# Finishing the early conditioning columns on ScalarE, and emitting each norm one tile later

## The chip, the cores and the metric

The kernel runs on 1 core of one Trainium2 chip. The metric is the device time of one execution in microseconds; before the change it is 2299.08 us (median of 3 runs, 2298.39 to 2300.27).

The core's engines run independently and meet at semaphores: TensorE (PE) multiplies, VectorE (DVE) and ScalarE (ACT) work elementwise, GpSimd (POOL) does little here, and SyncE (SP) issues nearly all the transfers. Each engine works through its own queue in order.

## The reference

Two decoder layers over 256 tokens of width 2048. Each layer has a token mixer (mLSTM in the first, forgetting attention in the second) and a SwiGLU network, each behind an RMSNorm that is modulated by a conditioning vector `c`:

```
cs = silu(c)
mod = cs @ ada_w[layer] + ada_b[layer]            # 6 vectors of 2048
sh1, sc1, g1, sh2, sc2, g2 = split(mod, 6)
h = rms_norm(x, norm_mix_w) * (1 + sc1) + sh1
x = x + g1 * mixer(h)
h = rms_norm(x, norm_ffn_w) * (1 + sc2) + sh2
x = x + g2 * swiglu(h)
```

A last RMSNorm closes it. All values are float32; matmuls use a value split into a high and a low part, three products for each.

## The kernel before

**Tiles.** Width 2048 is cut into 16 k-tiles of 128 partitions. `hT[:, k]` holds the modulated norm of k-tile `k`, transposed, as high and low parts for 256 tokens. A "unit" is 512 columns of the first projection `w_in`, over a range of k-tiles: `unit(i, ka, kb, ...)`, line 805. It fetches 1024 KB of weights (four k-tiles, `fetch`, L254), ACT casts them to the high part `hi` (L263), DVE subtracts for the low part `lo` (L264), and PE does 24 matmuls (L290 to L292), 12 for each half of the pair. Finished banks are copied out by `keep` (L800) and copied back as a start value (L812).

**Conditioning.** `mod` is computed by DVE, since `ada_w` would be used for only one row. For each of the 192 columns blocks `ada_tile` fetches 1024 KB and multiplies and sums it against `cs` in one instruction (L195) into one column of `acc`. `set_mods` adds the bias and, for a scale, multiplies by the norm's weight (L183 for a scale column, L189 for a shift column); the result stands in `mods`.

**The early stage.** The first norm needs scale (`SC1`) and shift (`SH1`) of layer 0, 32 products, before the first projection can use all of `hT`. So the kernel spreads these over the first units. The generator `early()` (L744) goes through k: product and column for `SC1`, a step ends; product and column for `SH1`, then the norm of tile k, a step ends. `norm_tile` (L378) consists of DVE `t` = x times scale times row norm (L382), ACT adds the shift and writes the high part of `hT` (L386), DVE writes the low part (L387). For k below 4 `norm_full` does the same with the full float32 value (L737, L741, L364, L365).

**Who advances it.** `upto(k)` runs the generator until k tiles of `hT` are emitted (`at[0]`), and `pace(1.0)` takes one step for each unit. Units 4 to 11 first use tiles 0 to 3, then units 0 to 11 tiles 4 to 7, then units 0 to 3 tiles 8 to 11. Each unit thus carries one product: two units make one k-tile of the norm.

**Order.** Up to L791 the instructions stand as written (a hand-kept order). After that a scheduler orders each engine's queue, so that an instruction may stand elsewhere than where the text emits it. Products and weights share a ring of five 1024 KB buffers (`rawp`); SP issues the next transfer when the buffer five back is free.

Of the kernel before, what the change touches and what calls it, by code (L numbers as in the profile page):

```python
# [12 lines left out]
AF = mybir.ActivationFunctionType  # L13
ALU = mybir.AluOpType
# [6 lines left out]
KT = D // P  # L21
# [10 lines left out]
def kernel(  # L32
# [5 lines left out]
    nc = tc.nc  # L38
# [45 lines left out]
    for j in range(3):  # L84
        nc.gpsimd.affine_select(
            out=sel, in_=sel, pattern=[[-1, 16]], compare_op=ALU.not_equal,
# [5 lines left out]
        out=mask, in_=mask, pattern=[[-1, P]], compare_op=ALU.is_ge,  # L92
# [74 lines left out]
    SH1, SC1, G1, SH2, SC2, G2 = range(6)  # L167


    for layer in range(2):  # L170
        for vec, nw in ((SC1, nw_mix), (SC2, nw_ffn)):
            b = adb[layer][:, 16 * vec : 16 * vec + 16]
            nc.vector.scalar_tensor_tensor(
                out=b, in0=b, scalar=1.0, in1=nw[layer], op0=ALU.add, op1=ALU.mult
            )

    def set_mods(layer, vec, k0, n):
        j = slice(16 * vec + k0, 16 * vec + k0 + n)
        m, a, b = mods[layer][:, j], acc[layer][:, j], adb[layer][:, j]
        if vec in (SC1, SC2):  # L180
            nw = (nw_mix if vec == SC1 else nw_ffn)[layer][:, k0 : k0 + n]
            if n == 1:
                nc.vector.scalar_tensor_tensor(  # L183
                    out=m, in0=a, scalar=nw, in1=b, op0=ALU.mult, op1=ALU.add
                )
                return
            nc.vector.tensor_tensor(m, a, nw, op=ALU.mult)
            a = m
        nc.vector.tensor_tensor(m, a, b, op=ALU.add)  # L189

    def ada_tile(layer, vec, k):
        j = 16 * vec + k
        raw = rawp.tile([P, D], F32, tag="raw", name=nm("ada"))
        nc.sync.dma_start(raw, ada_w[layer, j])
        nc.vector.scalar_tensor_tensor(  # L195
            out=raw, in0=raw, scalar=1.0, in1=cs, op0=ALU.mult, op1=ALU.mult,
            accum_out=acc[layer][:, j : j + 1],
        )
# [545 lines left out]
    def early():  # L744
        for k in range(KT):
            for vec in (SC1, SH1):
                ada_tile(0, vec, k)
                if k == 0 and vec == SC1:
                    row_scale()
                set_mods(0, vec, k, 1)  # L750
                if vec == SC1:
                    yield
            if k < 4:
                norm_full(k)
            else:
                norm_tile(k, 0, SC1, SH1)
            at[0] = k + 1
            yield

    at = [0]  # L760
    gen = early()
# [576 lines left out]
```

## Time and profile before

| | |
|---|---|
| median of 3 runs | 2299.08 us |
| profiled execution, own time | 2300.83 us |
| its span | 2299.0 us |
| PE busy | 2275.4 us |
| DVE busy | 1612.9 us |
| ACT busy | 1122.8 us |
| granted PE clock | 0.999 |

The profile shows one execution. A row of the timeline gives the start, the duration, the engine, the line, the operation with its output and inputs, the shape, and in brackets the idle time before it and what ended that. `x2` joins two equal instructions that follow each other; starts of successive rows may lie closer than the durations, since an engine begins an instruction before the last has written all its results. Stretches of time are given from the start of the span; the early stage ends near 193 us.

### The profile page before, as it was taken

Reading aid. Unit: us, or ns where it says so; the run is one execution under the profiler, and the core shown is the slowest. Engines: PE = TensorE matmul, PEld = TensorE weight load, DVE = VectorE, ACT = ScalarE, POOL = GpSimd, SP = SyncE. Lnnn points to the kernel's source line nnn. Section 1 sums busy time; section 2 is a strip of 40 time slices with the busy share of each in tenths; the row PEclk is TensorE's granted clock in tenths of the full one; section 3 lists DMA queues with packets and bytes.
Section 4 is the critical chain, followed back from the end, with each engine's and each line's share of the span. In section 5 each row is a group of like instructions: output and inputs, shape, how many; then the busy total and the mean of one; then the engine's idle time right before and its main releaser. Section 6 shows DMA issues by size and latency. Waiting matters only on the chain.

```text
span 2299.0 us, 26543 instructions
## 1 busy us (share of the span) xinstructions
PE 2275.4 (99%) x10376; PEld 1861.0 (81%) x10376; DVE 1612.9 (70%) x1829; ACT 1122.8 (49%) x1488; POOL 15.6 (1%) x40
## 2 busy tenths in 40 slices
PE   8999999999999999999999999999999999999998
PEld 4777878888888888888878888888888888888886
DVE  5998788878887878865687777777655554544554
ACT  3778664555543344444555444455444433444443
POOL 0000000000000000000000000000000000000000
PEclk9999999999999999999999999999999999999999
DMA  9998989798989889985667878775766555555552
GB/s 348 364 368 320 355 313 362 271 345 325 331 331 336 323 337 337 342 293 188 215 243 285 300 259 288 255 275 186 250 241 222 191 191 198 189 187 195 193 196 105
DMA packets 89090, 623.92 MB, mean 271 GB/s; under 512 B 10034, under 2 KB 10482, under 8 KB 14596
## 3 DMA queue, kind: packets, MB, share of 16 engines
q1 hardware_dynamic: 87552, 617.79, 74.3%
q0 software_dynamic: 1264, 4.29, 0.5%
q8 instruction: 81, 1.33, 0.2%
q14 instruction: 45, 0.37, 0.0%
q10 hardware_dynamic: 148, 0.14, 0.0%
HBM read 620.05 MB, written 2.13 MB: 271 GB/s over the span
## 4 chain that ended last, share of the span: by engine, by line
PE 88%; DVE 6%; DMA 3%; ACT 2%; issue 1%; SPq 0%; ACTq 0%; DVEq 0%
PE mm L292 25%; PE mm L291 25%; PE mm L290 25%; PE mm L273 5%; DVE ada L195 3%; PE mm L276 2%; DVE lo L264 2%; DMA ada<-in_ada_w_dram 2%; PE aux L347 1%; ACT hi L263 1%; DMA raw<-in_w_in_dram 1%; DMA slot<-in_w_in_dram 1%; PE aux L945 0%; PE aux L485 0%; PE aux L1144 0%
## 5 line engine op out<-in xcount | busy, mean ns | idle before, releaser
L264 DVE TENSOR_TENSOR lo<-raw,hi 128x1024 fp32r<-128x1024 f32 x764 | 926.9, 1223 | 556.8 <-ACT hi L263 556.2
L263 ACT CAST hi<-raw 128x1024 fp32r<-128x1024 f32 x764 | 797.1, 1053 | 920.3 <-PE mm L292 816.9
L291 PE MATMUL mm<-lo,hT 128*128 128x512 f32 x1840 | 718.3, 390 | 5.3 <-DVE lo L264 5.3
L290 PE MATMUL mm<-hi,hT 128*128 128x512 f32 x1840 | 719.3, 393 | 0.0
L292 PE MATMUL mm<-hi,hT 128*128 128x512 f32 x1840 | 718.1, 390 | 0.0
L195 DVE SCALAR_TENSOR_TENSOR ada<-ada,cs 128x2048 f32<-128x2048 f32 x192 | 438.9, 2286 | 49.2 <-DMA ada<-in_ada_w_dram 49.2
L291 PEld LDWEIGHTS mm<-lo,hT 128*128 128x128 f32 x1840 | 345.7, 188 | 80.1 <-DVE lo L264 10.2
L292 PEld LDWEIGHTS mm<-hi,hT 128*128 128x128 f32 x1840 | 345.4, 188 | 72.7 <-issue 0.5
L290 PEld LDWEIGHTS mm<-hi,hT 128*128 128x128 f32 x1840 | 345.3, 188 | 70.9 <-ACT hi L263 0.5
L290 PE MATMUL mm<-hi,slot 128*128 128x512 f32 x960 | 375.1, 391 | 0.2 <-ACT slot L978 0.2
L291 PE MATMUL mm<-lo,slot 128*128 128x512 f32 x960 | 374.4, 390 | 0.0
L292 PE MATMUL mm<-hi,slot 128*128 128x512 f32 x960 | 374.4, 391 | 0.0
L290 PEld LDWEIGHTS mm<-hi,slot 128*128 128x128 f32 x960 | 180.3, 188 | 37.7 <-ACT slot L978 0.8
L292 PEld LDWEIGHTS mm<-hi,slot 128*128 128x128 f32 x960 | 180.2, 188 | 37.6 <-issue 0.7
L291 PEld LDWEIGHTS mm<-lo,slot 128*128 128x128 f32 x960 | 180.2, 188 | 37.0
L273 PE MATMUL mm<-hT,hi 128*128 128x512 f32 x512 | 181.7, 402 | 0.6 <-DVE slot L359 0.6
L276 PE MATMUL mm<-hT,lo 128*128 128x256 f32 x512 | 138.3, 280 | 0.0
L273 PEld LDWEIGHTS mm<-hT,hi 128*128 128x128 f32 x512 | 94.4, 188 | 20.5 <-DVE slot L359 0.9
L276 PEld LDWEIGHTS mm<-hT,lo 128*128 128x128 f32 x512 | 96.6, 189 | 3.0
L800 ACT ACTIVATE slot<-mm 128x512 f32<-128x512 f32 x78 | 45.0, 593 | 33.9 <-PE mm L292 31.1
L435 ACT ACTIVATE t<-X 128x512 f32<-128x512 f32 x32 | 20.2, 631 | 39.2 <-DVE X L430 39.2
L1085 ACT ACTIVATE slot<-mm 128x512 f32<-128x512 f32 x44 | 25.4, 598 | 15.0 <-PE mm L292 13.8
(207 smaller groups left out, 980.5 us busy)
## 6 DMA issues: line engine op xcount, KB each, us to landing
ada<-in_ada_w_dram SPq DMA_DIRECT2D x192, 1024.0 KB, 6.5
raw<-in_gate_up_dram SPq DMA_DIRECT2D x176, 1024.0 KB, 4.9
raw<-in_down_dram SPq DMA_DIRECT2D x88, 1024.0 KB, 4.9
raw<-in_fox_in_dram SPq DMA_DIRECT2D x48, 1024.0 KB, 5.0
raw<-in_w_in_dram SPq DMA_DIRECT2D x44, 1024.0 KB, 7.3
raw<-in_w_out_dram SPq DMA_DIRECT2D x16, 1024.0 KB, 5.8
raw<-in_fox_out_dram SPq DMA_DIRECT2D x16, 1024.0 KB, 4.9
slot<-in_w_in_dram SPq DMA_DIRECT2D x16, 256.0 KB, 12.1
```

The lines of the kernel that those rows point to most:

```text
L195: nc.vector.scalar_tensor_tensor(out=raw, in0=raw, scalar=1.0, in1=cs, op0=ALU.mult, op1=ALU.mult, accum_out=acc[layer][:, j : j + 1],)
L263: nc.scalar.copy(hi, raw[:, j : j + 2, :])
L264: nc.vector.tensor_tensor(lo, raw[:, j : j + 2, :], hi.bitcast(F32), op=ALU.subtract)
L273: nc.tensor.matmul(ps, hi, rhs, start=first, stop=last, skip_group_check=True)
L276: nc.tensor.matmul(ps[:, T:], lo, rhs[:, :T], start=False, stop=False, skip_group_check=True)
L290: nc.tensor.matmul(ps, a, hi, start=first, stop=False, skip_group_check=True)
L291: nc.tensor.matmul(ps, a, lo, start=False, stop=False, skip_group_check=True)
L292: nc.tensor.matmul(ps, b, hi, start=False, stop=last, skip_group_check=True)
L347: nc.tensor.transpose(ps[:, j * T + t * P : j * T + (t + 1) * P], src[:, t, (2 * i + j) * P : (2 * i + j + 1) * P], ident,)
L435: nc.scalar.activation(t512(), X[:, t, 512 * i : 512 * (i + 1)], AF.Square, accum_out=self.ss[:, t, i : i + 1],)
L800: nc.scalar.activation(SP[i][:, t, :], banks[t], func)
L1085: nc.scalar.activation(sg[:, t, :], banks[t], AF.Silu)
```

## The change

It does two things. `set_mods` for a single column (which only `early()` asks for) gives the operation to ACT: one activation with the norm's weight as scale and the bias as bias, or the bias alone, in place of one DVE instruction. And for k from 4 on `early()` emits the norm of tile k at the start of the next tile, ahead of that tile's scale product; `at[0]` then counts it. Tile 15's norm is emitted after the loop as a step of its own. Lines after 183 move by 1 and after 748 by 5 in the changed kernel (L264 becomes L265, L382 becomes L383, L800 becomes L805).

```
--- before.py
+++ after.py
@@ -180,12 +180,13 @@
         if vec in (SC1, SC2):
             nw = (nw_mix if vec == SC1 else nw_ffn)[layer][:, k0 : k0 + n]
             if n == 1:
-                nc.vector.scalar_tensor_tensor(
-                    out=m, in0=a, scalar=nw, in1=b, op0=ALU.mult, op1=ALU.add
-                )
+                nc.scalar.activation(m, a, AF.Identity, bias=b, scale=nw)
                 return
             nc.vector.tensor_tensor(m, a, nw, op=ALU.mult)
             a = m
+        elif n == 1:
+            nc.scalar.activation(m, a, AF.Identity, bias=b)
+            return
         nc.vector.tensor_tensor(m, a, b, op=ALU.add)
 
     def ada_tile(layer, vec, k):
@@ -744,6 +745,9 @@
     def early():
         for k in range(KT):
             for vec in (SC1, SH1):
+                if vec == SC1 and k > 4:
+                    norm_tile(k - 1, 0, SC1, SH1)
+                    at[0] = k
                 ada_tile(0, vec, k)
                 if k == 0 and vec == SC1:
                     row_scale()
@@ -752,10 +756,11 @@
                     yield
             if k < 4:
                 norm_full(k)
-            else:
-                norm_tile(k, 0, SC1, SH1)
-            at[0] = k + 1
+                at[0] = k + 1
             yield
+        norm_tile(KT - 1, 0, SC1, SH1)
+        at[0] = KT
+        yield
 
     at = [0]
     gen = early()
```

**DVE, one tile.** The queue of DVE at tile 5 before; `ada` is the product, `mods` the column, `t` and `hT` the two DVE halves of the norm, `lo` the low part of weights, and the brackets name the engines waited for.

```order
L195 SCALAR_TENSOR_TENSOR ada_478,acc_124<-ada_478,cs 128x2048 [waits DMAHW5_49]
L183 SCALAR_TENSOR_TENSOR mods_122<-acc_124,prm 128x1 [waits DVE_49]
L382 SCALAR_TENSOR_TENSOR t_96_525<-slot_131,mods_122,R 128x256 [waits DVE_49]
L264 TENSOR_TENSOR lo_487<-raw_484,hi_486 128x1024 [waits DMAHW6_49,PE_49,Activation_49]
L264 TENSOR_TENSOR lo_491<-raw_484,hi_490 128x1024 [waits PE_49,Activation_49]
L195 SCALAR_TENSOR_TENSOR ada_521,acc_124<-ada_521,cs 128x2048 [waits DMAHW7_49]
L189 TENSOR_TENSOR mods_122<-acc_124,prm 128x1 [waits DVE_49]
L387 SCALAR_TENSOR_TENSOR hT<-t_96_525,mods_122,hT 128x256 [waits Activation_49]
L264 TENSOR_TENSOR lo_534<-raw_531,hi_533 128x1024 [waits DMAHW0_49,PE_49,Activation_49]
```

The same place after the change:

```order
L196 SCALAR_TENSOR_TENSOR ada_478,acc_124<-ada_478,cs 128x2048 [waits DMAHW5_49]
L383 SCALAR_TENSOR_TENSOR t_104_564<-slot_131,mods_122,R 128x256 [waits Activation_49]
L265 TENSOR_TENSOR lo_487<-raw_484,hi_486 128x1024 [waits DVE_49,DMAHW6_49,PE_49,Activation_49]
L265 TENSOR_TENSOR lo_491<-raw_484,hi_490 128x1024 [waits DVE_49,PE_49,Activation_49]
L196 SCALAR_TENSOR_TENSOR ada_521,acc_124<-ada_521,cs 128x2048 [waits DMAHW7_49]
L388 SCALAR_TENSOR_TENSOR hT<-t_104_564,mods_122,hT 128x256 [waits DVE_49,Activation_49]
L265 TENSOR_TENSOR lo_530<-raw_527,hi_529 128x1024 [waits DMAHW0_49,PE_49,Activation_49]
```

The two `mods` rows have left the queue. `t` and `hT`, which the text emits after both products, stand directly behind the first and the second one, as before, and `t` now waits for ACT.

**ACT, the same tile.** Before, from the copies out of two banks to the casts of two weight groups:

```order
L800 ACTIVATE slot_541<-mm_439 128x512 [waits DMAHW1_49,PE_49]
L800 ACTIVATE slot_541<-mm_440 128x512 [waits PE_49]
L698 COPY X<-aux_753 128x512 [waits PE_49]
L386 ACTIVATE hT<-t_96_525,mods_122 128x256 [waits DVE_49]
L263 CAST hi_533<-raw_531 128x1024 [waits DMAHW0_49,Activation_49]
L263 CAST hi_537<-raw_531 128x1024 [waits Activation_49]
L800 ACTIVATE slot_584<-mm_482 128x512 [waits DMAHW3_49,PE_49]
L800 ACTIVATE slot_584<-mm_483 128x512 [waits PE_49]
```

After:

```order
L183 ACTIVATE mods_122<-acc_124,prm 128x1 [waits DVE_49]
L264 CAST hi_486<-raw_484 128x1024 [waits DMAHW6_49]
L264 CAST hi_490<-raw_484 128x1024
L805 ACTIVATE slot_537<-mm_435 128x512 [waits DMAHW1_49,PE_49]
L805 ACTIVATE slot_537<-mm_436 128x512 [waits PE_49]
L699 COPY X<-aux_757 128x512 [waits PE_49]
L188 ACTIVATE mods_122<-acc_124,prm 128x1 [waits DVE_49]
L387 ACTIVATE hT<-t_104_564,mods_122 128x256 [waits Activation_49]
L264 CAST hi_529<-raw_527 128x1024 [waits DMAHW0_49]
L264 CAST hi_533<-raw_527 128x1024
```

Each column stands in ACT's queue ahead of two casts, and waits there for DVE's product.

**DVE, tiles 7 and 8.** After the change, where units 0 to 11 begin (`lo_720` belongs to unit 0; `slot_1471` and `slot_1477` are gate weights):

```order
L383 SCALAR_TENSOR_TENSOR t_136_709<-slot_131,mods_122,R 128x256 [waits Activation_49]
L265 TENSOR_TENSOR lo_667<-raw_664,hi_666 128x1024 [waits DVE_49,DMAHW6_49,PE_49,Activation_49]
L265 TENSOR_TENSOR lo_671<-raw_664,hi_670 128x1024 [waits DVE_49,PE_49,Activation_49]
L196 SCALAR_TENSOR_TENSOR ada_701,acc_124<-ada_701,cs 128x2048 [waits DMAHW7_49]
L196 SCALAR_TENSOR_TENSOR ada_713,acc_124<-ada_713,cs 128x2048 [waits DMAHW0_49,DVE_49]
L388 SCALAR_TENSOR_TENSOR hT<-t_136_709,mods_122,hT 128x256 [waits DVE_49,Activation_49]
L657 TENSOR_TENSOR slot_1471<-g_raw,slot_1471 128x8x4 [waits DMASW3_49,Activation_49]
L383 SCALAR_TENSOR_TENSOR t_155_813<-slot_132,mods_122,R 128x256 [waits Activation_49]
L657 TENSOR_TENSOR slot_1471<-g_raw,slot_1471 128x8x4 [waits Activation_49]
L657 TENSOR_TENSOR slot_1477<-g_raw,slot_1477 128x8x4 [waits Activation_49] x2
L265 TENSOR_TENSOR lo_720<-raw_717,hi_719 128x1024 [waits DMAHW1_49,PE_49,Activation_49]
L265 TENSOR_TENSOR lo_724<-raw_717,hi_723 128x1024 [waits PE_49,Activation_49]
```

Before, the second product of tile 7 was followed by the norm of tile 7 and then the weights of unit 0. Now the first product of tile 8 stands ahead of both, as it does in SP's queue; from here to tile 15 weights and products are shifted by one product, and the last units of the early stage come without one between them.

More of the change, by code (lines that the diff above doesn't have):

```diff
@@ L182, in set_mods @@
             if n == 1:
-                nc.vector.scalar_tensor_tensor(
-                    out=m, in0=a, scalar=nw, in1=b, op0=ALU.mult, op1=ALU.add
-                )
+                nc.scalar.activation(m, a, AF.Identity, bias=b, scale=nw)
                 return
@@ L188, in set_mods @@
             a = m
+        elif n == 1:
+            nc.scalar.activation(m, a, AF.Identity, bias=b)
+            return
         nc.vector.tensor_tensor(m, a, b, op=ALU.add)
@@ L746, in early @@
             for vec in (SC1, SH1):
+                if vec == SC1 and k > 4:
+                    norm_tile(k - 1, 0, SC1, SH1)
+                    at[0] = k
                 ada_tile(0, vec, k)
@@ L754, in early @@
                 norm_full(k)
-            else:
-                norm_tile(k, 0, SC1, SH1)
-            at[0] = k + 1
+                at[0] = k + 1
             yield
+        norm_tile(KT - 1, 0, SC1, SH1)
+        at[0] = KT
+        yield
     at = [0]
```

## The prediction

> **What bounds the kernel now.** I read the busy time by stage first, then the waits of VectorE (DVE) in the early stage, then one tile of that stage instruction by instruction on DVE and ScalarE (ACT).
>
> ```profile
> 146.00:193.00 47.00, 45.48 (x198) 36.32 (x196) 42.44 (x49) 33.78 (x52) 0.00 (x0) 1.00 0.97 361
> 193.00:226.00 33.00, 31.61 (x138) 25.19 (x136) 26.59 (x38) 28.68 (x45) 0.30 (x1) 1.00 0.85 304
> 226.00:300.00 74.00, 73.92 (x336) 59.85 (x337) 58.80 (x70) 47.37 (x69) 0.00 (x0) 1.00 0.89 345
> ...
> 300.00:400.00 100.00, 99.66 (x451) 77.54 (x450) 90.37 (x120) 55.98 (x87) 1.90 (x4) 1.00 0.89 342
> ```
>
> The columns are the stretch, its length, busy TensorE (PE), weight loads, DVE, ACT, GpSimd, then the granted PE clock, the DMA share and GB/s. From 226 to 400 us PE has next to no gaps, so a delay of PE before that passes through undiminished, and what comes later starts from PE's results. The change works in the early stage (to 193 us), where PE, DVE (42.4 of 47) and DMA (0.97) are all near full. Which of them sets the pace is seen in one tile:
>
> ```profile
> 157.37 2.36 DVE L264 TENSOR_TENSOR lo<-raw,hi 128x1024 fp32r<-128x1024 f32 x2 [0.46 <-ACT hi L263]
> 159.64 2.29 DVE L195 SCALAR_TENSOR_TENSOR ada<-ada,cs 128x2048 f32<-128x2048 f32 x1
> 161.85 0.08 DVE L195 DVE_READ_ACCUMULATOR ada<-ada,cs 128x1 f32 x1
> 161.97 0.22 DVE L183 SCALAR_TENSOR_TENSOR mods<-acc,prm 128x1 f32<-128x1 f32 x1
> 162.23 0.49 DVE L382 SCALAR_TENSOR_TENSOR t<-slot,mods,R 128x256 f32<-128x256 f32 x1
> 162.63 2.35 DVE L264 TENSOR_TENSOR lo<-raw,hi 128x1024 fp32r<-128x1024 f32 x2
> 164.91 2.29 DVE L195 SCALAR_TENSOR_TENSOR ada<-ada,cs 128x2048 f32<-128x2048 f32 x1
> 167.12 0.08 DVE L195 DVE_READ_ACCUMULATOR ada<-ada,cs 128x1 f32 x1
> 167.24 0.16 DVE L189 TENSOR_TENSOR mods<-acc,prm 128x1 f32<-128x1 f32 x1
> 167.97 0.48 DVE L387 SCALAR_TENSOR_TENSOR hT<-t,mods,hT 128x256 fp32r<-128x256 f32 x1 [0.58 <-ACT hT L386]
> 168.91 2.36 DVE L264 TENSOR_TENSOR lo<-raw,hi 128x1024 fp32r<-128x1024 f32 x2 [0.45 <-ACT hi L263]
> ```
>
> A tile takes 168.91 - 157.37 = 11.54 us. DVE runs without a pause except 0.58 us (for ACT's half of the norm) and 0.45 us (for the next cast, which stands behind that half in ACT's queue). No wait is for a DMA, and PE waits for DVE, once a tile:
>
> ```profile
> DVE lo L264 <- ACT hi L263: 11.6, 14, 5.9
> DVE hT L387 <- ACT hT L386: 6.9, 12, 0.6
> ...
> 181.74 0.50 PE L291 MATMUL mm<-lo,hT 128*128 128x512 f32 x1 [0.37 <-DVE lo L264]
> 187.33 0.39 PE L291 MATMUL mm<-lo,hT 128*128 128x512 f32 x1
> 192.09 0.39 PE L292 MATMUL mm<-hi,hT 128*128 128x512 f32 x1
> ```
>
> The last two rows are the first and last of 22 matmuls: 4.76 / 21 = 0.227 us each, so the 48 of a tile (two weight groups) take 10.9 us of 11.54. PE has about 0.64 us of slack a tile; the pace is the loop DVE to ACT to DVE.
>
> **The change on that loop.** Per tile two small operations leave DVE (0.22 and 0.16 us) and stand in ACT's queue. The built order decides what follows. Although the text now emits the norm a tile later, the scheduler puts its two DVE halves back where they were: `t` directly behind the first conditioning, `hT` directly behind the second. Both now need ACT's result. And in ACT's queue each conditioning stands ahead of the two casts of the next weight group. ACT's present order, and prices:
>
> ```profile
> 158.18 1.07 ACT L800 ACTIVATE slot<-mm 128x512 f32<-128x512 f32 x2
> 159.15 1.11 ACT L812 COPY mm<-slot 128x512 f32<-128x512 f32 x2
> 160.18 2.01 ACT L263 CAST hi<-raw 128x1024 fp32r<-128x1024 f32 x2
> ...
> 167.43 0.51 ACT L386 ACTIVATE hT<-t,mods 128x256 fp32r<-128x256 f32 x1 [1.86 <-DVE mods L189]
> 167.85 1.98 ACT L263 CAST hi<-raw 128x1024 fp32r<-128x1024 f32 x2
> ...
> L263 ACT CAST hi<-raw 128x1024 fp32r<-128x1024 f32 x52 | 51.9, 1047 | 3.8 <-DMA raw<-in_w_in_dram 3.8
> L711 ACT ACTIVATE rstd<-mm,eps_t 128x2 f32<-128x2 f32 x1 | 0.3, 262 | 2.3 <-PE mm L706 2.3
> L375 ACT ACTIVATE warm<-eps_t 128x1 f32<-128x1 f32 x1 | 0.2, 210 | 0.0
> ...
> 13.22 0.20 ACT L376 ACTIVATE warm<-warm 128x1 f32<-128x1 f32 x1
> 13.33 0.57 ACT L698 COPY X<-aux 128x512 f32<-128x512 f32 x1
> ```
>
> Today the casts at 160.18 run 2.5 us before DVE wants them (162.63). With the conditioning ahead of them they cannot start before DVE's accumulator is read. No row has this ACT operation with a scale and a bias from a column; the nearest are 0.20 to 0.26 us (128x1, 128x2). I take 0.21, the same size. ACT lets the next instruction start 0.11 us after a small one starts (13.22 to 13.33), and crossing engines takes 0.03 to 0.04 us (L189 ends 167.40, L386 starts 167.43).
>
> *First half*, in us from 157.37. The accumulator is read at 4.56. ACT conditions 4.60 to 4.81. DVE's `t` starts at 4.84, against 4.86 now, so handing over costs nothing by itself. The cast starts at 4.71 and ends 1.04 later, at 5.75; `lo` starts at 5.78 instead of 5.26. **Cost 0.52 us.**
>
> *Second half.* `lo`, conditioning product and accumulator take 4.57 as now, to 10.35. ACT conditions 10.39 to 10.60, does its half of the norm 10.63 to 11.14, and DVE's half starts at 11.17 (10.60 now). The cast behind it starts 0.42 after the norm's start (167.43 to 167.85), at 11.05, ends at 12.09, `lo` at 12.13 against 11.54. **Cost 0.07 us more.** The period becomes about 12.13.
>
> ACT's other work fits: casts, two copies out and two copies in end near 8.8 us, before the second conditioning at 10.39. If it did not, `t` or `hT` would slip by the excess. DMA moves the same bytes in a longer period.
>
> *The join.* The generator now needs one extra step to complete tile 7, and that step carries the product for the scale of tile 8. So SP issues that 1024 KB ahead of the next weights, and DVE multiplies twice in a row. From there to tile 15 each weight group stands behind one more product, half a tile. What it is worth follows from these rows:
>
> ```profile
> 93.17 2.35 DVE L264 TENSOR_TENSOR lo<-raw,hi 128x1024 fp32r<-128x1024 f32 x2
> 104.87 2.35 DVE L264 TENSOR_TENSOR lo<-raw,hi 128x1024 fp32r<-128x1024 f32 x2
> ...
> 185.72 2.35 DVE L264 TENSOR_TENSOR lo<-raw,hi 128x1024 fp32r<-128x1024 f32 x2
> 192.00 2.36 DVE L264 TENSOR_TENSOR lo<-raw,hi 128x1024 fp32r<-128x1024 f32 x2 [0.45 <-ACT hi L263]
> ```
>
> At the join DVE does 104.87 - 93.17 = 11.70, less 2.27 for the `lo` pair that moves behind, 9.43 us now. In the new order tile 7's norm is done under tile 8's product, without its 0.58 wait: product to 4.60, product to 6.89, norm half to 7.33; ACT conditions at 6.93, does three small gate casts, and the weight cast runs about 7.45 to 8.50, `lo` at 8.53. **Saves 0.9 us.** At the end the last early weight group (185.72 now) comes behind tile 15's second half: 192.00 - 185.72 = 6.28, less the pair's 2.27, **4.0 us later.**
>
> The first four tiles are conditioned in a hand-kept order. For tile 0 both conditionings queue behind ACT's copy ending at 20.75, so PE starts some 0.84 us later; the wait for tile 2 absorbs it, and costs that much if it were gone:
>
> ```profile
> 20.17 0.58 ACT L698 COPY X<-aux 128x512 f32<-128x512 f32 x1 [0.27 <-PE aux L695]
> 21.21 7.32 PE L786 MATMUL mm<-slot,t 128*128 128x512 f32 x12 [1.08 <-ACT t L741]
> 38.08 5.42 PE L786 MATMUL mm<-slot,t 128*128 128x512 f32 x12 [0.97 <-ACT t L741]
> ```
>
> **Sum.** First halves: tiles 4 to 7 and 9 to 15, 11 x 0.52 = 5.7. Second halves: all but tile 7, 11 x 0.07 = 0.8. Join -0.9, end +4.0: `lo` of the last early group 9.6 us late. PE took it at 187.33, though its first half was ready at 185.72 + 1.22 = 186.94, so PE is late by 9.2 to 9.3. After that PE runs back to back in both kernels but for two waits that a DVE now ahead of PE might lose:
>
> ```profile
> 218.80 0.50 PE L291 MATMUL mm<-lo,hT 128*128 128x512 f32 x1 [0.48 <-DVE lo L264]
> ...
> 226.09 0.50 PE L291 MATMUL mm<-lo,hT 128*128 128x512 f32 x1 [1.00 <-DVE lo L264]
> ```
>
> They hang on the gate chain, which starts from PE and so slips with it; of 1.48 us I give back 0.3. Between 300 and 340 us the new order has three more ACT table loads among exponentials and sigmoid copies. One costs 1.28 us:
>
> ```profile
> 324.53 1.28 ACT L906 ACT_TABLE_LOAD   x1
> ```
>
> Bounds 0 and 3.8 us; I take 0, since the order leaves some 20 PE matmuls and eight score products between score and use, and ACT is busy 56 of 100 us there. Total **+9.0 us**: 2300.83 becomes 2309.8 for the profiled execution, whose own time is 1.75 above the median of the runs; from that median, 2299.08, it is **2308.1 us**.
>
> The Trainium skill, "ScalarE: Activation LUTs", Rules for kernel authors, says multiplies and adds belong on VectorE and budgets about 0.3 us for each activation with a pointer bias; by that price each half costs 0.09 more, 22 x 0.09 = 2.0, and the time would be an estimated 2310.1. The rows at 0.20 to 0.26 lie lower, and the sum keeps 0.21.
>
> **Rivals.** *The half tile is made good* in the stage 193 to 226, where DVE (26.6 of 33) and ACT (28.7) have room: 4.0 - 0.9 = 3.1 us come back, +5.9, 2305.0. For it: DVE has no product left between the last two early groups. Against: PE is already back to back there, and lateness of PE can only be paid by its waits, 1.48 us in all.
>
> *The casts are not held up* (they would have to be done before the conditioning): only second halves, join and end remain, 0.8 - 0.9 + 4.0 - 0.4 = +3.5, 2302.6, within what can be told from no change. Against: ACT works its queue in order, as 167.43 shows, where it idles 1.86 us with a cast behind.
>
> *Relief of DVE decides, and the kernel is faster.* Place: DVE from 55 to 193 us. If ACT answers while DVE has other work, each tile loses 0.26 (161.97 to 162.23) and 0.16 us from the binding engine: 11 x 0.42 = 4.6 us, 2294.5; PE's slack of 0.64 a tile lets it through. It decides if the handing over takes under about 0.25 us and the casts are ready. The deferral in the text speaks for it, the built order against: at eleven tiles of twelve DVE needs the answer at once. The Trainium skill, "Perfetto Trace Analysis", Optimizing Scalar/DVE Operations, says that work may be moved to ScalarE when DVE is saturated, which would give this result. Here DVE idles 11.6 + 6.9 us for ACT in the stage, so by the trace it is not saturated but waiting for the engine that gets the work.
>
> *It costs more*: 0.26 us per conditioning (22 x 0.05 = 1.1) and half the table loads (1.9): 2311.1.
>
> *The change does nothing measurable*, because the scheduler undoes the deferral and ACT's extra work hides: 2299.
>
> **How the numbers follow.** Forecast 0.50, half tile made good 0.19, costs more 0.11, casts not held up 0.09, faster 0.08, nothing 0.03. A measurement of this kernel tells about 0.2% (4.6 us) from no change, so faster 0.08, same 0.12, slower 0.80. The range runs from 2302.5 (casts not held up) to 2312 (all unknown costs near their upper ends) and leaves out little more than the faster and the unchanged case.
>
> **What would show it.** In the new profile: the period between every second `lo` pair near 12.1 us; a wait of some 0.5 us of `lo` for the cast in the first half, beside the old two in the second; ACT idle ahead of both conditionings, for DVE; PE idle about 1.2 us a tile and several us at the join near 100 us; the last early group near 195 us; PE gapless after some 235 us. It would be wrong if the casts stood done when DVE comes, if ACT's operation took far less or more than 0.2 us, or if DVE ran the deferred norm under the next product.

## The result, and the profile after

The changed kernel takes 2320.27 us (median of 6 runs, 2317.15 to 2324.09) against 2299.12 us of the kernel before in 6 runs of the same series: ratio 1.0095, 95% interval 1.0082 to 1.0109. That is 21.2 us slower; 9.0 were forecast, with 2312.0 as the upper end. The profiled execution takes 2319.71 us with a span of 2317.9, 18.9 us more than the profiled one of before.

The busy time by stretch, of the changed kernel, with the columns as before (stretch, length, PE, weight loads, DVE, ACT, GpSimd, granted clock, DMA share, GB/s):

```profile
146.00:193.00 47.00, 44.02 (x182) 33.00 (x181) 38.82 (x39) 34.55 (x58) 0.00 (x0) 1.00 0.90 343
...
300.00:400.00 100.00, 97.18 (x425) 74.42 (x424) 87.27 (x120) 61.94 (x97) 1.90 (x4) 0.97 0.84 315
400.00:500.00 100.00, 95.64 (x431) 78.31 (x430) 78.81 (x96) 50.14 (x70) 0.00 (x0) 1.00 0.79 293
```

In the early stage PE is busy for 44.0 of 47 us (45.5 before); that it has more gaps was forecast. The surprise is in the last two rows: PE has 2.8 us of gaps between 300 and 400 us, at a clock below 1, and 4.4 us between 400 and 500. Before it had 0.3 in each of the two.

**One tile of the early stage** on DVE, from one second `lo` to the next (the lines have moved by one):

```profile
159.03 2.36 DVE L265 TENSOR_TENSOR lo<-raw,hi 128x1024 fp32r<-128x1024 f32 x2 [0.46 <-ACT hi L264]
161.31 2.28 DVE L196 SCALAR_TENSOR_TENSOR ada<-ada,cs 128x2048 f32<-128x2048 f32 x1
...
164.06 0.48 DVE L383 SCALAR_TENSOR_TENSOR t<-slot,mods,R 128x256 f32<-128x256 f32 x1 [0.46 <-ACT mods L183]
165.00 2.36 DVE L265 TENSOR_TENSOR lo<-raw,hi 128x1024 fp32r<-128x1024 f32 x2 [0.46 <-ACT hi L264]
167.28 2.29 DVE L196 SCALAR_TENSOR_TENSOR ada<-ada,cs 128x2048 f32<-128x2048 f32 x1
...
170.47 0.48 DVE L388 SCALAR_TENSOR_TENSOR hT<-t,mods,hT 128x256 fp32r<-128x256 f32 x1 [0.90 <-ACT hT L387]
171.41 1.22 DVE L265 TENSOR_TENSOR lo<-raw,hi 128x1024 fp32r<-128x1024 f32 x1 [0.45 <-ACT hi L264]
```

The period is 171.41 - 159.03 = 12.38 us (11.54 before, 12.13 forecast). The waits are the forecast ones: for ACT's conditioning, for the cast in both halves, and 0.90 instead of 0.58 for ACT's half of the norm. The first half takes 5.97 us instead of 5.26, the second 6.41 instead of 6.28. The sizes come from ACT. Its two groups between 60 and 200 us (count, busy time, mean ns of one, idle before):

```profile
L183 ACT ACTIVATE mods<-acc,prm 128x1 f32<-128x1 f32 x11 | 4.3, 387 | 17.7 <-DVE ada L196 17.7
L188 ACT ACTIVATE mods<-acc,prm 128x1 f32<-128x1 f32 x12 | 3.5, 295 | 22.0 <-DVE ada L196 22.0
```

and what follows one of them on ACT's timeline in the tile above:

```profile
163.64 0.39 ACT L183 ACTIVATE mods<-acc,prm 128x1 f32<-128x1 f32 x1 [1.72 <-DVE ada L196]
163.93 1.98 ACT L264 CAST hi<-raw 128x1024 fp32r<-128x1024 f32 x2
```

The conditioning with scale and bias columns takes 0.39 us, with a bias column alone 0.29, and the cast behind the first starts 0.29 us after the start of the conditioning, not 0.11.

**The join**, on PE:

```profile
99.34 0.39 PE L293 MATMUL mm<-hi,hT 128*128 128x512 f32 x1
103.12 1.22 PE L291 MATMUL mm<-hi,hT 128*128 128x512 f32 x2 [3.39 <-ACT hi L264]
...
104.97 0.63 PE L293 MATMUL mm<-hi,hT 128*128 128x512 f32 x1
```

and by stretch, the time in which the trace has the lower clock:

```profile
102.90:109.70 6.80, 6.54 (x15) 4.71 (x16) 5.25 (x6) 3.08 (x6) 0.00 (x0) 0.50 0.77 293
```

PE waits 3.39 us for unit 0's first cast, which stands behind one more product, and then its granted clock is 0.50 for 6.8 us: rows of 0.39 become rows of 0.63. The trace of before has the full clock from 25 us to its last 4. On DVE, then ACT:

```profile
93.17 2.36 DVE L265 TENSOR_TENSOR lo<-raw,hi 128x1024 fp32r<-128x1024 f32 x2 [0.46 <-ACT hi L264]
...
103.10 2.36 DVE L265 TENSOR_TENSOR lo<-raw,hi 128x1024 fp32r<-128x1024 f32 x2 [0.50 <-ACT hi L264]
...
108.57 0.48 DVE L388 SCALAR_TENSOR_TENSOR hT<-t,mods,hT 128x256 fp32r<-128x256 f32 x1 [0.90 <-ACT hT L387]
...
99.09 0.60 ACT L805 ACTIVATE slot<-mm 128x512 f32<-128x512 f32 x1 [0.47 <-PE mm L293]
...
102.03 1.99 ACT L264 CAST hi<-raw 128x1024 fp32r<-128x1024 f32 x2
...
108.03 0.51 ACT L387 ACTIVATE hT<-t,mods 128x256 fp32r<-128x256 f32 x1
```

From `lo` to `lo` over the join it is 103.10 - 93.17 = 9.93 us. The cast of unit 0 stands behind ACT's copies of the bank ahead, which wait for PE. DVE's next wait for the norm is 0.90 us, as in every tile: here PE's stall and the half clock don't come back to DVE. PE, 6.0 us late behind the stall against the kernel before, is 5.2 late 18 us further on; its slack takes the stall up until `lo`, then 5.2 late as well, sets its pace again.

**Behind 300 us**, PE's waits in two stretches of the changed kernel (total, times, longest):

```profile
PE aux L401 <- DVE slot L962: 1.2, 1, 1.2
PE mm L293 <- DVE slot L984: 1.1, 1, 1.1
```

```profile
PE mm L557 <- DVE hT L511: 3.5, 2, 1.8
PE aux L486 <- DVE slot L475: 0.7, 1, 0.7
```

The first two fall into 340 to 360 us, in the mLSTM heads, the last two into 430 to 460, in the bridge from the mixer's output to the FFN.

**Where the time comes from.** PE does 8400 matmuls of split products in every version, in nearly the same order. The n-th of one kernel's trace starts so much later than the n-th of before (us; the first column is its start in before):

| start before | what lies there | changed kernel |
|---|---|---|
| 53.0 (`lo`, first of the stage) | start | -3.2 |
| 89.7 | ahead of the join | -2.4 |
| 106.0 | behind the join | +6.0 |
| 201.4 | end of the early stage | +10.3 |
| 231.2 | two former waits gone | +8.8 |
| 299.7 | ahead of the heads | +8.7 |
| 362.6 | behind the heads | +13.5 |
| 520.0 | behind the bridge | +17.6 |
| 2244.8 | end | +19.0 |

Up to 300 us the changed kernel is 8.7 us late, which looks like the forecast; the other 10.3 us come where the forecast saw PE without a gap, 8.8 of them between 300 and 520 us.

### The profile page after: what moved, and what is told of

It reads as the page before. It is cut to its first block, busy times and chain, and to the rows that moved or that the text cites. A ratio compares the mean times of both kernels' runs of the same rounds, so it can differ in the third digit from the quotient of the medians.

```text
span 2317.9 us, 26573 instructions
## 1 busy us (share of the span) xinstructions
PE 2284.4 (99%) x10376; PEld 1864.6 (80%) x10376; DVE 1608.5 (69%) x1797; ACT 1134.6 (49%) x1523; POOL 15.6 (1%) x40
## 4 chain that ended last, share of the span: by engine, by line
PE 87%; DVE 6%; ACT 3%; DMA 2%; issue 2%; SPq 0%; ACTq 0%; DVEq 0%
PE mm L293 24%; PE mm L292 24%; PE mm L291 24%; PE mm L274 5%; DVE ada L196 3%; PE mm L277 2%; DMA ada<-in_ada_w_dram 2%; DVE lo L265 2%; ACT hi L264 1%; PE aux L348 1%; PE mm L791 1%; PE aux L950 0%; PE aux L486 0%; PE aux L1149 0%; PE mm L557 0%
## 5 line engine op out<-in xcount | busy, mean ns | idle before, releaser
L265 DVE TENSOR_TENSOR lo<-raw,hi 128x1024 fp32r<-128x1024 f32 x764 | 926.6, 1222 | 566.6 <-ACT hi L264 563.3
L264 ACT CAST hi<-raw 128x1024 fp32r<-128x1024 f32 x764 | 796.9, 1053 | 913.9 <-PE mm L293 819.9
L805 ACT ACTIVATE slot<-mm 128x512 f32<-128x512 f32 x78 | 43.9, 590 | 25.8 <-PE mm L293 23.1
## 6 DMA issues: line engine op xcount, KB each, us to landing
slot<-in_w_in_dram SPq DMA_DIRECT2D x16, 256.0 KB, 10.5
```

Source lines behind the costliest of these rows:

```text
L264: nc.scalar.copy(hi, raw[:, j : j + 2, :])
L265: nc.vector.tensor_tensor(lo, raw[:, j : j + 2, :], hi.bitcast(F32), op=ALU.subtract)
L805: nc.scalar.activation(SP[i][:, t, :], banks[t], func)
```

## The experiments

Each kernel was timed in 5 rounds or more beside the kernel before on the same chip. "Late" is always a start in its trace minus that in the profiled execution of before.

### The two halves of the change apart

Conditioning on ACT alone (the norm emitted as before):

```diff
-                nc.vector.scalar_tensor_tensor(
-                    out=m, in0=a, scalar=nw, in1=b, op0=ALU.mult, op1=ALU.add
-                )
+                nc.scalar.activation(m, a, AF.Identity, bias=b, scale=nw)
...
+        elif n == 1:
+            nc.scalar.activation(m, a, AF.Identity, bias=b)
+            return
```

> Only the conditioning moves to ACT; the norm is emitted where it stood before, so that the half tile at the join and the later order of the work stay as before. Theory (the changed kernel's extra time is two things: a longer loop in the early stage, and, from 300 us on, another order of the later work that comes with the half tile at the join): tiles of 12.38 us instead of 11.54, 12 x 0.84 = 10.1 us up to 193 us, less about 1.4 that PE's two waits near 220 us give back, so +8.7 with the start of before, or +5.5 if the start comes 3.2 us earlier as it did in the changed kernel: 2304.6 to 2307.8; 19 ACT table loads; no half clock; the PE's lateness stays constant from 240 us to the end. Rival 1 (it is the conditioning on ACT, or being late at all, that costs the 10 us after 300 us): 2315 or more, with growing lateness near 350 and 440 us. Rival 2 (the prediction's price, 0.21 us for the ACT operation): period 12.13, 2305.9, told from the theory by the period.

Measured: 2307.3 us against 2298.49, ratio 1.0043 (1.0031 to 1.0056). The period on DVE, from rows one tile apart:

```profile
161.50 2.36 DVE L265 TENSOR_TENSOR lo<-raw,hi 128x1024 fp32r<-128x1024 f32 x2 [0.46 <-ACT hi L264]
...
173.88 2.36 DVE L265 TENSOR_TENSOR lo<-raw,hi 128x1024 fp32r<-128x1024 f32 x2 [0.46 <-ACT hi L264]
```

12.38 us again. The first `lo` comes 3.2 us early, the last early group's 6.5 late: 9.7 us in twelve tiles. From 206 us to the end PE's lateness stays between 5.9 and 6.5. So the conditioning costs the loop what the changed kernel's period says, and it costs nothing behind it. Rival 1 falls, and so does the price of 0.21.

Deferral alone (conditioning on DVE as before):

```diff
+                if vec == SC1 and k > 4:
+                    norm_tile(k - 1, 0, SC1, SH1)
+                    at[0] = k
                 ada_tile(0, vec, k)
...
-            else:
-                norm_tile(k, 0, SC1, SH1)
```

> Only the later emission of the norm; the conditioning stays on DVE. Theory: the tile's period stays 11.54, the last early weight group stands one half tile later (+3.1 after the join's saving), 1.3 of it regained near 220 us; then the order of the work after 300 us, which is that of the changed kernel with its 22 table loads, costs the same 10.2 us as there: 2299.1 + 3.1 - 1.3 + 10.2 = 2311, between 2309 and 2313, with half clock near 100 us and near 352 us. Rival 1 (the later cost comes with ACT's conditioning): 2300 to 2303, lateness constant after 240 us.

Measured: 2308.57 us, ratio 1.0049 (1.0036 to 1.0061), 0.4 us under the lower end of what was expected. From its first `lo`, 4.1 us early, it loses 5.3 us up to 206 us, regains 1.5 near 225, loses 4.8 at the heads and 3.8 at the bridge, and wins 0.8 later. The half clock comes at 101.6 and 347.3 us. The two halves add up to nearly the whole, 8.8 + 10.1 = 18.9 of 21.2 us.

A text that defers every norm but tile 7's is built to the order of before on PE, DVE, ACT and SP, row for row: the deferral moves nothing but the join, and what follows from the join.

### The join

The generator skips one step behind the join, so that only unit 0's weights stand behind one more product:

```diff
     def upto(k):
         while at[0] < k:
             next(gen)
+            if at[0] == 8 and k == 8:
+                owe[0] -= 1.0
```

With the conditioning on DVE:

> The later emission of the norm with the conditioning on DVE, but the generator skips one step behind the join, so that only unit 0's weights stand behind one product more and everything behind them has its former place; 19 table loads, the later order of before. It prices the join alone: PE's wait of some 3 us near 100 us and the half clock behind it. Theory: DVE is back in its former place one unit later, PE has about 0.64 us of slack in each of the 8 tiles left, 5.1 us, and takes both up before 193 us: 2299 to 2300, no change. Rival (the stall and the slow clock are carried to the end): +3.4 to +6.8, 2302.5 to 2306.

Measured: 2303.04 us, ratio 1.0022 (1.0013 to 1.0031). The rival holds: the join with the skipped step costs 4.5 us. `lo` is 3.7 us early up to the join, 2.1 early just behind it, and 0.6 late from the next tile to 193 us, flat: 4.4 us, lost in two steps. DVE, then ACT:

```profile
89.43 2.35 DVE L264 TENSOR_TENSOR lo<-raw,hi 128x1024 fp32r<-128x1024 f32 x2
...
100.48 4.63 DVE L264 TENSOR_TENSOR lo<-raw,hi 128x1024 fp32r<-128x1024 f32 x4 [0.40 <-ACT hi L263]
...
110.83 0.49 DVE L387 SCALAR_TENSOR_TENSOR hT<-t,mods,hT 128x256 fp32r<-128x256 f32 x1 [3.32 <-ACT hT L386]
...
107.98 0.60 ACT L806 ACTIVATE slot<-mm 128x512 f32<-128x512 f32 x1 [4.69 <-PE mm L292]
...
110.29 0.51 ACT L386 ACTIVATE hT<-t,mods 128x256 fp32r<-128x256 f32 x1
```

From `lo` to `lo` over the join it is 11.05 us, with both products between; the old order's share was 9.43. That is the first step, 1.6 us: the casts stand behind ACT's copies, which wait for PE to end the unit before. (In the deferral alone it is 11.08 us; in the changed kernel 9.93, since PE ends the unit before sooner after that `lo`: ACT's first copy starts 5.92 us behind it, not 7.32.) The second shows how PE's stall gets into DVE's loop, which has no slack: ACT copies unit 0 out of PSUM when PE is done with it, 3.1 us and 3.4 us of half clock late. The norm half stands behind that copy in ACT's queue, and DVE waits 3.32 us for it instead of 0.58. This second step comes with the skipped step, which puts the weights of two units together, so that ACT reaches the norm half only behind the copy. In the changed kernel and in the deferral alone a product and the norm half stand between the two units, the norm half runs ahead of the copies, and DVE waits the usual 0.90 and 0.58 us.

The whole change with the step skipped:

> The whole change, but with the generator's step skipped behind the join: conditioning on ACT, norm emitted a tile later, half tile given back after unit 0; 19 table loads, the later order of before. Theory: as with the conditioning alone, 2304.6 to 2307.8, so 12 to 15 us less than the changed kernel, since the order after 300 us is that of before. Rival (the changed kernel's loss comes from the conditioning, the stall at the join and the slow clock, not from the later order): 2315 to 2320.

Measured: 2311.3 us, ratio 1.0056 (1.0043 to 1.0068), 3.5 us above the expected range: the cost of this join was missing in it, 9.93 us from `lo` to `lo`, and then a wait of 3.64 us for the norm half instead of 0.90. It is 9.0 us under the changed kernel, and its lateness stays at 8.7 to 8.8 from 206 to 650 us.

To see what the clock is worth in this join, PE was kept busy in its wait, on top of the skipped step and with the conditioning on DVE:

```diff
             settle(1)
+            if i == 0 and ka == 4:
+                idle = abank()
+                for _ in range(14):
+                    tc.keep_in_program_order(
+                        nc.tensor.matmul(idle, hT[:, 0, :P], hT[:, 0, :], start=True, stop=True)
+                    )
```

> The run that prices the join alone (half tile given back behind unit 0, conditioning on DVE), with 14 matmuls without use put on PE ahead of unit 0's first one, 14 x 0.227 = 3.2 us, so that PE is busy in the 3.1 us in which it waits for the cast. They write a spare PSUM bank that nobody reads; a few transposes of x move for it. Theory (of the 4.4 us that this join costs, what the 3.4 us of half clock cost PE, 1.7 us, is carried on, since ACT's copy out of unit 0's banks waits for PE, the norm stands behind it and DVE waits for the norm): the granted clock stays at 1.00 and the time is 1.7 us less, 2301.3. Rival 1 (the stall alone is carried, the slow clock is lost in PE's slack): 2303. Rival 2 (all of it is the clock): 2298.5 to 2299.5.

Measured: 2298.61 us against 2297.79, ratio 1.0001 (0.9992 to 1.001). The added matmuls on PE's timeline, then the stretch around the join:

```profile
96.09 3.34 PE L827 MATMUL aux<-hT 128*128 128x512 f32 x14
...
99.40 0.71 PE L290 MATMUL mm<-hi,hT 128*128 128x512 f32 x2
```

```profile
94.00:110.00 16.00, 16.00 (x75) 13.19 (x75) 12.50 (x21) 12.77 (x22) 0.00 (x0) 1.00 0.98 381
```

The clock stays at 1.00, and DVE's `lo` loses 1.6 us at the join instead of 4.4. The time is rival 2's, but the run isn't clean: the transposes of x that moved let PE end the unit ahead of the join sooner, and the cast of unit 0 starts at 98.28 instead of 99.41. Of the 2.8 us, 1.1 may be that; the rest, 1.6, is the size expected for the clock. How it divides exactly stays open.

### The order behind 300 us

In the changed kernel's DVE order the same background products (`ada`, 2.3 us each, conditioning for later stages) stand at other places than before. In the bridge, after and then before:

```profile
430.68 0.69 DVE L430 TENSOR_TENSOR t<-mm,slot 128x512 f32<-128x512 f32 x1 [2.92 <-PE mm L293]
431.29 2.28 DVE L196 SCALAR_TENSOR_TENSOR ada<-ada,cs 128x2048 f32<-128x2048 f32 x1
...
433.50 0.69 DVE L431 TENSOR_TENSOR X<-X,t 128x512 f32<-128x512 f32 x1
...
438.52 2.28 DVE L196 SCALAR_TENSOR_TENSOR ada<-ada,cs 128x2048 f32<-128x2048 f32 x1
...
440.73 0.69 DVE L511 TENSOR_TENSOR hT<-t,hT 128x512 fp32r<-128x512 f32 x1
```

```profile
420.31 2.28 DVE L195 SCALAR_TENSOR_TENSOR ada<-ada,cs 128x2048 f32<-128x2048 f32 x1
...
422.82 1.36 DVE L497 TENSOR_SCALAR t<-aux,mods 128x128 f32<-128x128 f32 x4 [0.21 <-PE aux L485]
...
426.22 2.29 DVE L195 SCALAR_TENSOR_TENSOR ada<-ada,cs 128x2048 f32<-128x2048 f32 x1
```

A product stands between the two halves of the last residual sum, another just ahead of the low half of `hT`, for which PE waits. Before, they stood where DVE waits for ACT or PE anyway: behind the first scaling, where it still waits 0.21 us for PE afterwards, and behind the second residual sum. Three kernels pin, one after the other, parts of the changed kernel's order to that of before (each pin only fixes the issue order on one engine):

```diff
+        if i == 7 and func == AF.Sigmoid:
+            for hd in (2, 3):
+                if hd in exps:
+                    tc.add_manual_dep(
+                        exps[hd].ins, e.ins.name,
...
             norm.scale(0, 0)
+            mark(65, norm.scaled)
...
             res(i, 1, tb[1])
+            mark(66, res.sum)
...
             norm.low(1, 0)
+            mark(67, norm.lowed)
...
+            if hd == 3:
+                mark(53, e)
...
+            if hd == 2:
+                mark(56, e)
```

The first piece puts the exponentials of heads 2 and 3 on ACT behind the sigmoid copies of the last unit. `mark(n, e)` puts the n-th background product on DVE behind the instruction `e`: in the bridge the first scaling, the second residual sum and the second low half, in the heads the last score product and the last low half of an output.

The first pin alone:

> The changed kernel, with one thing pinned: the two sigmoid copies of the last mixer unit are issued on ACT ahead of the exponentials of the last two heads, as in the kernel before, so that the three extra table loads near 330 us go (19 loads in all). All else of the changed kernel's order up to 300 us stays, and the bridge near 440 us keeps the products where the changed kernel has them. Theory (the extra table loads make the mLSTM heads late, PE waits for them near 350 us and its clock is halved there): PE's lateness stays near 8.7 us from 240 to 400 us instead of going from 8.7 to 13.5; no half clock near 352 us; the bridge still costs some 4 us: 4.8 less than the changed kernel, 2315.5, between 2314.5 and 2317. Rival (the loads are hidden, and the 4.8 us come from elsewhere in the later order): 2319 to 2321.

Measured: 2316.14 us against 2299.03, ratio 1.0073 (1.0061 to 1.0086). It is in the range, but for less than was said: PE's lateness grows from 7.9 to 10.9 in the heads, 3.0 instead of 4.8. The half clock near 352 us is gone. PE's waits are not:

```profile
PE mm L557 <- DVE hT L511: 3.4, 2, 1.8
PE mm L291 <- ACT slot L994: 1.5, 1, 1.5
PE aux L961 <- DVE slot L995: 1.4, 1, 1.4
```

So the place of the exponentials, with the three table loads and the slow clock, is worth 1.8 of the 4.8 us; the pin moves other instructions of the heads too, so what the loads alone cost isn't shown. The rest of its gain, 3.2 us in the trace, lies behind 600 us, where nothing was pinned (1.8 won, 1.4 lost in the changed kernel); executions with the order of before behind the early stage differ there by up to 1.8 us too, and it stays unexplained.

With the bridge pinned too:

> As the one before, and the three background products of the first bridge are pinned to the places that they have in the kernel before (behind the first scaling, behind the second residual sum, behind the third affine step) instead of between the two halves of the residual sum, between the affine step and the low half, and between the scaling and the affine step. Theory (each product of 2.3 us that stands inside the chain from the last residual sum to hT makes PE wait there): the 4.1 us near 440 us go too: 2311.4, between 2310 and 2313, the time of the change with its half tile given back, 2311.3. Rival (the placing is no cause, the bridge is late for what comes before it): 2315 to 2317.

Measured: 2313.24 us, ratio 1.0061 (1.0047 to 1.0074), 0.2 over the expected range. PE loses nothing in the bridge (11.6 us late ahead of it and behind it; 10.9 and 14.9 without this pin): the products' places are the cause.

With the two products in the heads pinned too:

> As the run with loads and bridge undone, and two more background products of DVE are pinned to the places that they have in the kernel before: the 53rd behind the second head's score products instead of between the two heads', the 56th behind both pairs of low halves of the third head's output instead of between them. Theory (PE's two waits near 352 us, 1.5 and 1.4 us, come from products of 2.3 us that stand inside the heads' chain on DVE): PE's lateness keeps its 8.6 us from 240 to 400 us instead of growing to 11.6: 2.9 us less than there, 2310.3, between 2309 and 2312. Rival (they come from the half tile itself, whatever the products do): 2313.

Measured: 2309.73 us against 2297.79, ratio 1.0045 (1.0031 to 1.0058). Between 308 and 460 us PE waits three times, for 0.2 us each. The lateness is 8.9 us at 271 and 9.0 at 520 us, 9.8 at the end (8.7, 17.6 and 19.0 in the changed kernel). The places of a few exponentials on ACT and of five products on DVE, 200 us and more behind the change, made 8.7 of the 8.8 us that it loses between 300 and 520 us. On the medians the time over before falls from 21.2 to 11.9 us. Being late is not the cause: in the eight other kernels here without these pins, all but the deferral alone, PE's lateness changes by at most 0.1 us between 300 and 520 us, whatever it is.

### The deferral that the text asks for

What if the norm really ran under the next product? With the conditioning on DVE, ACT's half was pinned behind the casts and DVE's half behind the product, except in tiles 7 and 15:

```diff
+                late = vec == SC1 and k > 4 and k != 8
+                if late:
+                    tail = norm_head(k - 1)
                 ada_tile(0, vec, k)
+                if late:
+                    tail()
+                    at[0] = k
```

`norm_head` does `t` and ACT's half, which it pins behind the ACT instruction written last; `tail` does DVE's half, pinned behind the product.

> The deferral that the change's text asks for, done so that the built order has it, with the conditioning on DVE as before: in tiles 4 to 6 and 8 to 14 ACT's half of the norm is pinned behind the casts of the weights that come next, and DVE's half behind the next product; tiles 7 and 15 as before, so that no half tile is lost at the join. 19 table loads, the later order of before. Theory (DVE's two waits for ACT, 0.58 and 0.45 us a tile, are what keeps the tile at 11.54 us, and both go): the period falls to PE's 10.9 to 11.2, 10 tiles by 0.35 to 0.6 = 3.5 to 6 us saved, and nothing behind 193 us takes it back: 2293 to 2295.5. Rival 1 (the DMA, busy 0.97 of the stage, is the next bound): within 1 us of before, 2298 to 2299. Rival 2 (the later order or a PE wait takes it back): 2298 or more with a shorter period.

Measured: 2299.18 us, ratio 0.9999 (0.999 to 1.0008): no change, but for neither rival's reason. The instruction written last was a copy, not the cast, so that ACT's half still stood ahead of the casts. ACT, then DVE:

```profile
154.73 0.51 ACT L753 ACTIVATE hT<-t,mods 128x256 fp32r<-128x256 f32 x1 [2.21 <-DVE mods L189]
...
156.21 2.36 DVE L264 TENSOR_TENSOR lo<-raw,hi 128x1024 fp32r<-128x1024 f32 x2 [1.51 <-ACT hi L263]
...
168.02 2.36 DVE L264 TENSOR_TENSOR lo<-raw,hi 128x1024 fp32r<-128x1024 f32 x2 [1.52 <-ACT hi L263]
```

DVE's wait for the norm had become a longer wait for the cast; the period is 11.81 us. The same with the conditioning on ACT:

> As the one before, with the conditioning on ACT too, each pinned behind the casts and emitted half a tile late, so that no engine waits for it: what the whole change could have been. It takes another 0.38 us a tile off DVE. Theory (with DVE's waits gone the period is set by PE or the DMA, so a lighter DVE brings nothing): within 1.5 us of the run with the conditioning on DVE. Rival (DVE is still the bound): another 10 x 0.38 = 3.8 us faster.

Measured: 2308.04 us, ratio 1.0036 (1.0023 to 1.0048), the time of the conditioning alone. It has the same fault, so it doesn't test its theory. In the next two the pin holds on to the last cast itself:

```diff
-        nc.scalar.copy(hi, raw[:, j : j + 2, :])
+        cast[0] = nc.scalar.copy(hi, raw[:, j : j + 2, :])
...
-        tc.keep_in_program_order(nc.scalar.activation(dst[:, :T], t1, AF.Identity, bias=b))
+        behind_casts(nc.scalar.activation(dst[:, :T], t1, AF.Identity, bias=b))
```

> The true deferral again, with the conditioning on DVE: in the run before ACT's half of the norm was pinned behind the instruction that happened to be written last, and still stood ahead of the casts, waiting 2.2 us for DVE with the casts behind it. Now it is pinned behind the last cast itself; the orders of DVE and PE are word for word those of that run. Theory: lo no longer waits for the cast (1.5 us a tile there), nor DVE's half for ACT; the period falls from 11.8 to PE's 10.9 to 11.2: 10 tiles by 0.35 to 0.6 against before, 2293 to 2295.5. Rival 1 (the DMA, busy 0.97 of the stage, sets the period as soon as DVE does not): 2298 to 2299.5, with waits for a DMA in the stage. Rival 2 (given back behind 193 us): 2298 or more with the shorter period.

> As late2, with the conditioning on ACT, each pinned behind the casts and emitted half a tile late, so that neither t nor the casts wait for it. It takes 0.38 us a tile off DVE. Theory (without DVE's waits the period is set by PE or by the DMA): within 1.5 us of late2. Rival (DVE is still the bound): 3.8 us faster than late2.

Measured: 2293.89 us with the conditioning on DVE, ratio 0.9978 (0.9968 to 0.9989), and 2293.28 with it on ACT, ratio 0.998 (0.9972 to 0.9989), against 2297.79. Both beat both kernels. Of the first, the stretch of the stage, and then DVE one tile apart:

```profile
146.00:193.00 47.00, 47.00 (x209) 38.93 (x208) 42.19 (x48) 35.19 (x54) 0.00 (x0) 1.00 0.97 373
```

```profile
150.62 2.36 DVE L276 TENSOR_TENSOR lo<-raw,hi 128x1024 fp32r<-128x1024 f32 x2 [0.49 <-ACT hi L275]
...
161.51 2.36 DVE L276 TENSOR_TENSOR lo<-raw,hi 128x1024 fp32r<-128x1024 f32 x2 [0.59 <-ACT hi L275]
```

The same of the second:

```profile
146.00:193.00 47.00, 47.00 (x209) 38.94 (x208) 40.21 (x41) 37.71 (x63) 0.30 (x1) 1.00 0.98 372
```

```profile
149.16 2.36 DVE L277 TENSOR_TENSOR lo<-raw,hi 128x1024 fp32r<-128x1024 f32 x2 [0.26 <-ACT hi L276]
...
160.04 2.36 DVE L277 TENSOR_TENSOR lo<-raw,hi 128x1024 fp32r<-128x1024 f32 x2 [0.27 <-ACT hi L276]
```

Periods of 10.89 and 10.88 us, PE busy for all 47. In these 47 us DVE is busy for 2 us less in the second, with the same period: with the waits gone, PE is the bound, and relieving DVE is worth nothing. The DMA moves 373 GB/s instead of 361, and PE doesn't wait for it in this stretch.

## Why the prediction was wrong

**The direction and the mechanism of the early stage** were right: DVE to ACT to DVE sets the pace, the conditioning stands ahead of the casts, the text's deferral is undone by the built order, PE passes the lateness on. Every wait named beforehand is in the profile. The sizes, counted from the first `lo` in each trace (at the end of the stage `lo` is 10.5 + 3.2 = 13.7 us late, PE 10.3 + 3.2 = 13.5):

| term of the sum | predicted | measured |
|---|---|---|
| first halves, 11 times | 0.52, 5.7 | 0.71, 7.8 |
| second halves, 11 times | 0.07, 0.8 | 0.13, 1.4 |
| join | -0.9 | 9.93 - 9.43 = 0.5 |
| end | 4.0 | 13.7 - 9.2 - 0.5 = 4.0 |
| given back at PE's two waits | -0.3 | -1.5 |
| PE took the last group later anyway | -0.3 | -0.2 |
| sum to 300 us | 9.0 | 12.0 |
| behind 300 us | 0 | 10.3 |

That PE's lateness at 300 us, 8.7, is so near the forecast of 9.0 is luck: the loss is 12.0 us, and the earlier start in this trace takes 3.2 off.

**"I take 0.21, the same size"** failed. The nearest rows were activations of the same few elements, but with at most one operand that is a column, or none; the price hangs on that: 0.39 with two, 0.29 with one. The cast's start at 0.11 behind a small instruction was taken from a row without columns as well; it is 0.29. The two make 2.7 us: the later cast 2.1 in the first halves, the longer conditioning ahead of the norm half 0.6 in the second ones. The Trainium skill's price in "ScalarE: Activation LUTs", Rules for kernel authors, about 0.3 us for an activation with a bias from a pointer, agrees with the 0.29; the prediction set it beside the sum and kept the lower rows.

**The join** was to save 0.9 us and cost 0.5: from `lo` to `lo` 8.53 us were forecast instead of 9.43, and it took 9.93, since ACT was not free for the cast before PE had ended a unit (99.09) and its banks were copied. That PE would idle "several us at the join" was said, and nothing was set down for it, rightly: the stall of 3.39 us and the slow clock cost nothing in `lo` behind the join. They do come back to DVE, 2.7 us (3.32 instead of 0.58), where the generator skips a step behind the join.

**"Three more table loads: 0 of 0 to 3.8"**: about 1.8 us, with the slow clock and whatever else the pin moved, within the bounds. **The start's 0.84** is there as 1.0: PE's first wait for `t` is 2.08 us in all eight traces with the conditioning on ACT and 1.08 in the six with it on DVE, and the wait for tile 2 (0.97 before) is gone in the changed kernel, as forecast. What the start costs as a whole can't be told, since it differs between executions: in all runs here the first `lo` comes 1.5 to 4.1 us sooner than in the profiled execution of before, also where the start is unchanged (4.1 in the deferral alone). So the profiled execution of before was a late one; of the 21.2 us between the medians its trace shows 19.

**"After that PE runs back to back in both kernels"** is the step that failed most: PE lost 10.3 us there. The order was read at the places of the change; behind it only the table loads were compared. Five products and a few exponentials had moved into the chains for which PE waits, and put back they give 8.7 us of it; another 1.4 us, behind 600 us, have no cause shown. The range had no term for that.

**The rivals.** "The casts are not held up" and "nothing" fell with the waits in the profile; "costs more" had a price nearer to that of a bias column, and half the table loads, and still ended 9 us short. "The half tile is made good" has a grain of truth: both of PE's waits near 220 us go, 1.5 us instead of 0.3. "Relief of DVE decides" fell in this kernel, and in its own best case too: where ACT's answer is hidden the time falls, but by as much with the conditioning left on DVE.

Of what would show it, the wait of 0.46 for the cast in the first half, ACT's idle time ahead of both conditionings (1.72) and PE's stall at the join are there; the period is 12.38 rather than 12.1, the last early group starts at 196.2 rather than 195, and PE is not gapless behind 235 us.

## What to carry to other kernels

Where a scheduler sets the order, a small edit is priced in two parts: its own place, and every place behind it where the built order differs, each read for what now stands inside a chain that PE waits for. A small instruction that moves to an in-order queue costs what stands behind it there, so put it behind the work that others wait for, and check in the built order that it stands there. A norm that is really deferred, with pins on the instructions it must follow, took the loop from 11.54 to 10.9 us and this kernel to 0.998 of its time; which engine did the small conditioning then made no difference.

## What was not expected of the hardware

PE's granted clock fell to 0.5 for 3.4 or 6.8 us at waits that are short against the kernel. At the join it came between 1.2 us ahead of the end of PE's wait (the run with the heads' products pinned) and 2.0 us after it (the deferral with the skipped step), and it needs no single long pause: in the changed kernel the stretch ahead of the second fall, and the slow one itself, are

```profile
348.70:352.10 3.40, 1.68 (x11) 0.95 (x9) 3.37 (x6) 1.82 (x4) 0.50 (x1) 1.00 0.93 373
352.10:358.90 6.80, 5.70 (x10) 3.33 (x11) 6.13 (x9) 1.48 (x4) 1.08 (x2) 0.50 1.00 382
```

PE was busy for half of the 3.4 us, and its longest pause there was 1.25. With the exponentials pinned, two pauses of 1.5 and 1.4 us in the heads, 3 us apart, brought no slow clock.

In every trace here the changes of the clock lie whole multiples of 3.413 us apart. In the changed kernel it falls at 102.9, rises at 109.7, falls at 352.1 and rises at 358.9 us: 2, 71 and 2 times 3.413. Cut on this grid into windows at full clock, up to 2280 us, the traces tell more than the pauses do. Nine windows had PE busy for 1.52 us or less, and all were followed by the slow clock; of ten with 1.6 to 1.75 us two were, and with more, none. (Busy time has modelled ends, so the border is rough.) A pause of 2.08 us near 20 us brought the slow clock in the run with the bridge pinned, where the whole pause fell into one window; in three other runs an edge of the grid cut the same pause, and it brought none.

The Trainium skill, "TensorE: Matmul & The Clock Gate", Part 1: The HAM clock gate, says that the clock halves after an idle window of about 3.4 us, that these windows run freely, and that as long a busy time brings it back. The grid and the lengths of the slow stretches agree; but here a window with PE busy for up to half of it was enough.
